# Keys, b's and receptances by token: 64x128 transposes in place of 64x64 products with an identity

## The chip, the cores and the metric

The kernel runs on one core of a Trainium2 chip. The metric is the device time of one execution in microseconds. A measurement is the median of several executions. Engines are called by the profile's names: PE is TensorE's matmul, PEld its weight load, DVE VectorE, ACT ScalarE, POOL GpSimd, SP SyncE, which issues most transfers.

## What is computed

One decoder block, for 16 meta tokens and 1024 tokens of width 1024: a half-step SwiGLU, a mixer with two branches (A: gated DeltaNet in chunks; B: RWKV-7), an output projection, another half-step SwiGLU, a norm. The change lies in branch B, whose reference is a recurrence over the tokens with one 64x64 state per head:

```python
def step(state, inp):
    r_t, w_t, k_t, v_t, a_t, b_t = inp
    sa = jnp.einsum('bhvk,bhk->bhv', state, a_t)
    state = state * w_t[:, :, None, :] + sa[..., None] * b_t[:, :, None, :] \
        + v_t[..., None] * k_t[:, :, None, :]
    return state, jnp.einsum('bhvk,bhk->bhv', state, r_t)
```

with `a_vec = -kk`, `b_vec = kk * a`, 16 heads of 64 channels.

## The kernel before

The kernel works in three parts: `ffn1`, `middle`, `ffn2`. `middle` holds both mixers. It takes the tokens in two segments (first 16 meta + 512 tokens, then 512) and the heads in eight groups `j`: two heads of branch B (128 partitions, one head in each half of them, `HS[0]` and `HS[1]`) and one head of branch A. So there are 16 iterations, 0 to 7 in segment 0 and 8 to 15 in segment 1. `schedule()` gives the order of the steps of an iteration; steps of three iterations stand side by side in it:

```python
REGULAR = "merge_blocks transitions operands+ inverses+ chains gates finish decay++ new_b++ new_a++"
```

That is the order in which the code is written. The framework's scheduler then gives each engine its own order, by data dependences, free buffers and its own idea of times; the projections (`pp`, three products per block of 128 rows) fill TensorE's order between the small products.

Branch B does not step through the tokens. It works on 8 chunks of 64 tokens (`NCB`, `CB`). `new_b` makes, with channels on the partitions, keys and b's scaled by decay (`BK`) and a-vectors and receptances scaled by decay (`AR`; `AR[:, :, 0]` is called "receptances" in the change's title, though it is made from `kkn`). `operands` multiplies them into the chunk matrices `LT` (tile `grb`), and turns them so that tokens are on the partitions:

- `bkt` (L1574): for each chunk, for `d` = 0, 1 and each head's half `h`, one 64x64 block of `BK` is multiplied with a 64x64 identity. The result goes to the partitions `HS[h ^ d]` of the bank `ps[d]`. ACT copies the two banks to `BKt` (L1577).
- `vp<-ck,AR` (L1342, in `run`): the same for `AR[..., 0, :]`, 16 products, copied to `at` (L1589); together with them, into the other half of the same two banks, 16 products `vp<-LT,Vs`, copied to `yb` (L1591).

`run` writes products of 64x64 blocks into up to two banks, one bank for blocks that stay on their half of the partitions and one for those that change it. `tok(i, h)` says on which half the tokens of chunk `i` of head `h` lie for the solve; `key(i, h)` is the other half. `transitions`, an iteration later, reads `BKt` and `at` block by block (tiles `xp`, `vp<-Vs,BKt`, `mp`, `np`), and `chains` runs the recurrences over the chunks (`p1`, `p2`, `pq`, `p3` for A, `b1` for B, `bq`). In segment 0 two more turns serve the meta tokens of branch A: `vmp` in `new_a` (L1483) and in `operands` (L1605), products of 16 columns with a 128x128 identity. The turns of A's full chunks (`vap` L1478, `ktp` L1600) are transposes already.

PSUM banks for these tiles come from the pool `mx`; `g.C(name)` is a slice of the constants' tile `ck`, and `g.sums` holds two 128x128 matrices (all ones, and ones in the two 64x64 blocks) by which column sums are taken.

## Time and profile before

| | us |
|---|---|
| median of 3 runs (2971.76 to 2984.48) | 2976.71 |
| the profiled execution | 2974.08 |
| its span, first to last instruction | 2972.3 |
| PE busy in the span | 2876.8 (97%) |
| DVE busy | 2208.8 (74%) |
| ACT busy | 1450.5 (49%) |
| POOL busy | 503.4 (17%) |
| mean granted TensorE clock | 0.993 |

In the rows that follow, `x64` is a number of instructions, `64*64` after an operation of TensorE is the part of the array that is used (rows by columns), and `64x64 f32` the operand. A busy time of a group counts overlapping instructions once. In the chain of work that ended last, the second number is the length of the piece.

### The profile page before, as it was taken

The page shows a single profiled execution, that of the slowest core. Times are in us where ns is not written, and L with a number is a line of the kernel's source. Part 1 is how long each engine was busy: PE and PEld are TensorE (multiplying, and loading weights), DVE is VectorE, ACT ScalarE, POOL GpSimd, SP SyncE. Part 2 cuts the span into 40 slices and gives each one's busy share as a digit, 9 for nine tenths or more (in the row PEclk, how much of TensorE's full clock was granted, in tenths as well). Part 3 has the DMA queues.
Part 4 walks back from the last instruction along what each step waited for, and adds up shares of the span by engine and source line. Part 5 has one row for each costly group of instructions (what it writes and reads, how often), then busy time and mean ns, then how long its engine had stood idle before and what let it go on. Part 6 is the DMA issues. An engine that isn't in the chain of part 4 may idle for free.

```text
span 2972.3 us, 63124 instructions
## 1 busy us (share of the span) xinstructions
PE 2876.8 (97%) x25720; PEld 2496.4 (84%) x25720; DVE 2208.8 (74%) x4121; ACT 1450.5 (49%) x2559; POOL 503.4 (17%) x578
## 2 busy tenths in 40 slices
PE   8999999999899999999998999999999999999998
PEld 8999999999878888888776777777777888888887
DVE  8666668776667877788878887778876766667886
ACT  6322234346555656565566556556644422223443
POOL 0332232323000000000000000001101032332431
PEclk9999999999999999999999999999999999999999
DMA  5333236553232322333232332333345332333763
GB/s 212 125 108 108 98 124 206 182 193 118 71 70 72 86 65 68 84 81 85 89 98 73 80 79 77 76 87 82 106 132 185 127 109 99 97 102 130 248 220 113
DMA packets 287907, 339.39 MB, mean 114 GB/s; under 512 B 172704, under 2 KB 181024, under 8 KB 287616
## 3 DMA queue, kind: packets, MB, share of 16 engines
q1 hardware_dynamic: 283600, 326.17, 36.0%
q0 software_dynamic: 2000, 6.56, 0.6%
q8 instruction: 202, 3.31, 0.5%
q10 hardware_dynamic: 2016, 2.63, 0.2%
q14 instruction: 89, 0.73, 0.1%
HBM read 267.63 MB, written 73.41 MB: 115 GB/s over the span
## 4 chain that ended last, share of the span: by engine, by line
PE 67%; DVE 19%; ACT 6%; issue 3%; DMA 3%; SPq 1%; POOL 0%; DVEq 0%; ACTq 0%; POOLq 0%
PE pg L521 25%; PE pp L315 15%; PE pd L742 10%; DVE w L164 3%; PE pwo L315 2%; PE pg L545 2%; DVE tb L1657 1%; DVE Xb L1659 1%; DVE form L164 1%; ACT w L163 1%; PE vp L1342 1%; DMA form<-frm 1%; PE mp L1342 1%; PE xp L1342 1%; PE np L1342 1%
## 5 line engine op out<-in xcount | busy, mean ns | idle before, releaser
L315 PE MATMUL pp<-uk,w 128*128 128x512 f32 (+2 forms) x4824 | 971.3, 347 | 13.8 <-DVE w L164 5.9
L315 PEld LDWEIGHTS pp<-uk,w 128*128 128x128 f32 x4824 | 745.4, 191 | 111.7 <-DVE w L164 14.7
L742 PE MATMUL pd<-form,w 128*128 128x256 f32 (+2 forms) x2904 | 437.3, 312 | 5.4 <-DVE w L164 5.2
L742 PEld LDWEIGHTS pd<-form,w 128*128 128x128 f32 x2904 | 402.7, 189 | 39.5 <-DVE w L164 7.3
L521 PE MATMUL pg<-bt,w 128*128 128x256 f32 (+2 forms) x2520 | 401.9, 318 | 3.1 <-DVE w L164 2.5
L521 PEld LDWEIGHTS pg<-bt,w 128*128 128x128 f32 x2520 | 360.2, 188 | 37.3 <-DVE w L164 3.8
L527 DVE TENSOR_TENSOR c<-c,pg 128x520 f32<-128x520 f32 (+1 forms) x280 | 189.4, 688 | 239.1 <-PE pg L521 215.8
L164 DVE TENSOR_TENSOR w<-wraw,w 128x1024 fp32r<-128x1024 f32 (+1 forms) x254 | 338.2, 1332 | 38.7 <-ACT w L163 37.1
L521 PE MATMUL pg<-b,w 128*128 128x256 f32 (+2 forms) x2160 | 348.1, 317 | 0.0
L163 ACT ACTIVATE w<-wraw 128x1024 fp32r<-128x1024 f32 (+1 forms) x254 | 266.9, 1052 | 164.1 <-PE pg L521 117.4
L521 PEld LDWEIGHTS pg<-b,w 128*128 128x128 f32 x2160 | 309.9, 188 | 28.3 <-DVE w L164 0.3
L163 ACT ACTIVATE w<-wrx 128x1024 fp32r<-128x1024 f32 (+1 forms) x64 | 58.4, 912 | 279.0 <-PE pg L521 239.2
L491 POOL TENSOR_TENSOR wrx<-wrx 128x512 f32<-128x512 f32 x38 | 52.5, 1381 | 612.8 <-DVE w22b L164 351.6
L164 DVE TENSOR_TENSOR form<-form 128x520 fp32r<-128x520 f32 (+1 forms) x152 | 145.8, 995 | 14.0 <-ACT form L163 13.8
L163 ACT ACTIVATE w<-wsum 128x768 fp32r<-128x768 f32 x96 | 75.6, 788 | 155.8 <-PE pd L742 117.1
L164 DVE TENSOR_TENSOR w<-wsum,w 128x768 fp32r<-128x768 f32 x96 | 112.9, 1181 | 37.3 <-ACT w L163 37.3
L163 ACT ACTIVATE form<-form 128x520 fp32r<-128x520 f32 (+1 forms) x152 | 93.8, 631 | 79.5 <-DMA form<-frm 73.4
L242 POOL TENSOR_TENSOR wsum<-wsum,wraw 128x768 f32<-128x768 f32 (+1 forms) x48 | 97.6, 2050 | 204.7 <-DMA wraw<-in_wdn 154.3
L1659 DVE TENSOR_TENSOR Xb<-Xb,tb 115x126 f32<-115x126 f32 (+22 forms) x496 | 125.2, 252 | 8.7
L1657 DVE TENSOR_TENSOR tb<-Ub,Xb 115x126 f32<-115x126 f32 (+22 forms) x496 | 124.5, 251 | 9.5 <-DMA Ub<-scr 2.0
L1466 DVE SCALAR_TENSOR_TENSOR acc<-xr,pk,acc 128x528 f32<-128x528 f32 (+1 forms) x144 | 109.0, 757 | 20.6 <-ACT acc L1462 19.9
L315 PE MATMUL pwo<-uk,w 128*128 128x512 f32 x384 | 95.3, 397 | 1.3 <-DVE uk L164 0.6
(439 smaller groups left out, 4421.4 us busy)
## 6 DMA issues: line engine op xcount, KB each, us to landing
wraw<-in_win SPq DMA_DIRECT2D x150, 512.0 KB
wraw<-in_wgu SPq DMA_DIRECT2D x44, 512.0 KB
wrx<-in_wgu SPq DMA_DIRECT2D x44, 512.0 KB
frm<-c SPq DMA_DIRECT2D x76, 260.0 KB
form<-frm SPq DMA_DIRECT2D x76, 260.0 KB
frm<-c SPq DMA_DIRECT2D x76, 256.0 KB
form<-frm SPq DMA_DIRECT2D x76, 256.0 KB
...
```

The costliest lines, as they stand in the source:

```text
L163: g.nc.scalar.activation(hi, src, AF.Copy)
L164: (eng or g.nc.vector).tensor_tensor(lo, src, hi.bitcast(F32), op=ALU.subtract)
L242: g.nc.gpsimd.tensor_tensor(s, x, y, op=ALU.add if r == 1 else ALU.subtract)
L315: g.last_product = g.nc.tensor.matmul(ps, lhsT=l, rhs=r, start=i == 0, stop=i == n - 1)
L521: nc.tensor.matmul(ps[:, c0 : c0 + cn], lhsT=l[:, x, k, :], rhs=r[:, k, y, c0 : c0 + cn], start=i == 0, stop=i == 3 * HK - 1)
L527: nc.vector.tensor_tensor(o, x, y, op=ALU.add)
L545: nc.tensor.matmul(ps[:, c0 : c0 + cn], lhsT=l[:, x, k, :], rhs=r[:, k, y, c0 : c0 + cn], start=i == 0, stop=i == 6 * HK - 1)
L742: nc.tensor.matmul(pd[:, c0 : c0 + cn], lhsT=wd[:, u, k - k0, :], rhs=x[:, v, c0 : c0 + cn], start=k + i == 0, stop=k == HF - 1 and i == 2)
L1342: g.nc.tensor.matmul(ps[e][HS[dst], c0 : c0 + CB], lhsT=l, rhs=r, start=True, stop=True)
L1466: nc.vector.scalar_tensor_tensor(acc[:, :n], xr[:, tap : tap + n], V("convw", ct * 4 + tap), acc[:, :n], op0=ALU.mult, op1=ALU.add)
L1657: nc.vector.tensor_tensor(tv, U[:, i, i + 1 :].unsqueeze(2).to_broadcast([npt, nt, ncc]), X[:, i, 0:ncc].unsqueeze(1).to_broadcast([npt, n ...
L1659: nc.vector.tensor_tensor(X[:, i + 1 :, 0:ncc], X[:, i + 1 :, 0:ncc], tv, op=ALU.add)
```

## The change

`BK` and `AR` lose the inner axis of two (b's and keys; a's and receptances). They become two runs of eight chunks with one more block of 64 columns between them, 17 blocks in all. POOL fills that block with three 64x64 copies per iteration, so that on the second head's half the chunks can also be taken in pairs that begin one block later. `turned` takes two neighbouring chunks of one half at a time, 64 rows by 128 columns, and transposes them into a 128x64 block: 16 transposes for `bkt`, 8 for `AR`. Bank `h` now holds head `h`. `place` and `turned_bk` find the blocks again in `transitions`. The two `vmp` products become transposes of 128 columns. The constant `bd` leaves `ck`; POOL makes the two matrices of `g.sums` with memsets, where DVE copied them.

```diff
@@ middle
-            nc.vector.tensor_copy(g.sums[x], g.C(x))
+            t = g.sums[x].bitcast(F32)
+            nc.gpsimd.memset(t, 0.0 if x == "bd" else 1.0)
+            if x == "bd":
+                for h in HS:
+                    nc.gpsimd.memset(t[h, h], 1.0)
...
+def place(i, h):
+    return (i - h) % NCB // 2
...
-def run(g, pool, name, *kinds):
-    ps, out, used = {}, [], [0, 0]
+def run(g, pool, name, *kinds, banks=()):
+    ps, out, used = dict(enumerate(banks)), [], [0, 0]
...
+def turned(g, ps, src, first):
+    for m in range(NCB // 2):
+        for h in range(2):
+            i = 2 * m + first[h]
+            g.nc.tensor.transpose(ps[h][:, m * CB : (m + 1) * CB], src[HS[h], i : i + 2].rearrange("p a m -> p (a m)"),
+                                  g.C("ident")[HS[h], HS[h]])
@@ new_b
-    BK = q.BK = st.tile([P, NCB, 2, CB], F32, name="BK", tag="BK")
-    nc.vector.tensor_tensor(BK[:, :, 1, :], ch3(k[:, fs], CB), ch3(EN[:, fs], CB), op=ALU.mult)
-    nc.vector.scalar_tensor_tensor(BK[:, :, 0, :], ch3(t1[:, fs], CB), -1.0, ch3(EN[:, fs], CB),
-                                   op0=ALU.mult, op1=ALU.mult)
-    AR = q.AR = st.tile([P, NCB, 2, CB], F32, name="AR", tag="AR", bufs=2)
-    nc.vector.tensor_tensor(AR[:, :, 0, :], ch3(kkn[:, fs], CB), ELx[:, :, 0:CB], op=ALU.mult)
+    BK = q.BK = st.tile([P, 2 * NCB + 1, CB], F32, name="BK", tag="BK")
+    ks, bs = BK[:, NCB + 1 :], BK[:, :NCB]
+    nc.vector.tensor_tensor(ks, ch3(k[:, fs], CB), ch3(EN[:, fs], CB), op=ALU.mult)
+    nc.gpsimd.tensor_copy(BK[HS[0], NCB], ks[HS[0], NCB - 1])
+    nc.vector.scalar_tensor_tensor(bs, ch3(t1[:, fs], CB), -1.0, ch3(EN[:, fs], CB), op0=ALU.mult, op1=ALU.mult)
+    nc.gpsimd.tensor_copy(BK[HS[1], NCB], bs[HS[1], 0])
+    AR = q.AR = st.tile([P, 2 * NCB + 1, CB], F32, name="AR", tag="AR", bufs=2)
+    nc.vector.tensor_tensor(AR[:, :NCB], ch3(kkn[:, fs], CB), ELx[:, :, 0:CB], op=ALU.mult)
+    nc.gpsimd.tensor_copy(AR[HS[1], NCB], AR[HS[1], 0])
@@ new_a (and the same in operands with kq[:, 0, 0:P])
-        nc.tensor.matmul(ps[:16, 0:P], lhsT=acc[:, 0:16], rhs=g.C("ident"), start=True, stop=True)
+        nc.tensor.transpose(ps[:, 0:P], acc[:, 0:P], g.C("ident"))
@@ operands
-    for i in range(NCB):
-        for d in range(2):
-            for h in range(2):
-                nc.tensor.matmul(ps[d][HS[h ^ d], i * CB : (i + 1) * CB], lhsT=BK[HS[h], i, d ^ (i & 1)],
-                                 rhs=ident[HS[h], HS[h]], start=True, stop=True)
-    for d in range(2):
-        nc.scalar.activation(BKt[:, :, d], ch3(ps[d], CB), AF.Copy)
+    turned(g, ps, BK, (0, 1))
+    turned(g, [p[:, FULL // 2 :] for p in ps], BK[:, NCB:], (0, 1))
+    for h in range(2):
+        nc.scalar.activation(BKt[:, :, h], ch3(ps[h], CB), AF.Copy)
...
+    banks = [g.mx.tile([P, 512], F32, name="vp", tag="mx") for _ in range(2)]
+    ps = [t[:, FULL // 2 :] for t in banks]
+    turned(g, ps, AR, (0, 1))
+    for h in range(2):
+        nc.scalar.activation(at[:, h * (NCB // 2) : (h + 1) * (NCB // 2)], ch3(ps[h], CB), AF.Copy)
...
-    pa, pr = run(g, g.mx, "vp", lambda i, h: (AR[HS[h], i, 0, :], ident[HS[h], HS[h]], h, tok(i, h)), vr)
-    for ps, cs in pa:
-        nc.scalar.activation(at[:, cs], ps, AF.Copy)
-    for ps, cs in pr:
+    for ps, cs in run(g, g.mx, "vp", vr, banks=banks)[0]:
         nc.scalar.activation(ch3(yb, CB)[:, cs], ps, AF.Copy)
@@ transitions (the blocks' new places)
+    def turned_bk(p, i, d):
+        h, s = p ^ d, d ^ (i & 1)
+        return BKt[HS[p], s * (NCB // 2) + place(i + s, h), h]
```

In the program order of each engine the change moves the following. In these rows numbers tell tiles of one name apart (after, `bkt_12167` and `bkt_12168` are the two banks), and `x8` counts products of the program.

TensorE in iteration 3 (segment 0), from the end of the small products for the meta tokens, before:

```order
L1808 MATMUL am_12422<-vnm,vkm 128x128
L1574 MATMUL bkt<-ck,BK 64x64 x32
L1815 MATMUL p_12427<-SA,kq 128x128
L1840 MATMUL b_12431<-SBs,mt 128x64
L315 MATMUL pp<-uk,w 128x512
L1342 MATMUL vp<-ck,AR 64x64 x16
L1342 MATMUL vp<-LT,Vs 64x64 x16
L1821 MATMUL p_12434<-rhA,Y_7680 128x128
L1840 MATMUL b_12436<-SBs,mt 128x64
```

and after:

```order
L314 MATMUL pp_12531<-uk_7559,w_12493 128x512
L1360 MATMUL bkt_12167<-ck_7211,BK_11563 128x64 x8
L314 MATMUL pp_12531<-uk_7603,w_12493 128x512
L1360 MATMUL bkt_12168<-ck_7211,BK_11563 128x64 x8
L1360 MATMUL vp_12188<-ck_7211,AR_11568 128x64 x4
L1838 MATMUL p1_12345<-SA_10946,kq_10297 128x128
L1863 MATMUL b1_12349<-SBs_12343,mt_7684 128x64
L314 MATMUL pp_12531<-uk_7603,w_12493 128x512
L1360 MATMUL vp_12189<-ck_7211,AR_11568 128x64 x4
L1350 MATMUL vp_12188<-LT_12058,Vs_11402 64x64 x7
```

Before, the 32 products stood together and mixed the two banks. The changed code writes the transposes of the two halves in turn; here all eight of bank 0 (the first head's half) come first and all eight of bank 1 behind a projection. The receptances' transposes stand four and four.

TensorE in iteration 10 (segment 1), behind the last `gra` of the same step, before:

```order
L1574 MATMUL bkt_19860<-ck_7211,BK_19374 64x64 x16
L1815 MATMUL p1_20033<-SA_18968,kq_18413 128x128
L315 MATMUL pp_20217<-uk_18047,w_20179 128x512
L1840 MATMUL b1_20037<-SBs_20031,mt_7684 128x64
L315 MATMUL pp_20217<-uk_18047,w_20179 128x512
L1574 MATMUL bkt_19861<-ck_7211,BK_19374 64x64 x16
L1342 MATMUL vp_19898<-ck_7211,AR_19377 64x64 x2
L1342 MATMUL vp_19899<-ck_7211,AR_19377 64x64 x2
```

and after:

```order
L1360 MATMUL bkt_20725<-ck_7211,BK_20236 128x64 x8
L1838 MATMUL p1_20874<-SA_19736,kq_19205 128x128
L314 MATMUL pp_21023<-uk_17893,w_20985 128x512
L1863 MATMUL b1_20878<-SBs_20872,mt_7684 128x64
L314 MATMUL pp_21023<-uk_17893,w_20985 128x512
L1360 MATMUL bkt_20726<-ck_7211,BK_20236 128x64 x8
L314 MATMUL pp_21023<-uk_17899,w_20985 128x512
L1360 MATMUL vp_20746<-ck_7211,AR_20241 128x64 x4
L314 MATMUL pp_21023<-uk_17899,w_20985 128x512
L1360 MATMUL vp_20747<-ck_7211,AR_20241 128x64 x4
```

Here two projections now stand between the second half of `bkt` and the two parts of `vp`, which had mixed before.

POOL in segment 1, one iteration's stretch from the copies that feed the inverses (`XA`) to the clearing of `Xb`, after (before, the same rows without the three 64x64 copies, and with `XA` behind the third `xr`):

```order
L1692 COPY XA<-Xc 32x4x32 [waits DMAHW6_49,Pool_49]
L1692 COPY XA<-Xc 32x4x32
L1449 COPY AR<-AR 64x64 [waits DVE_49]
L1480 COPY xr<-carA 128x3 [waits Pool_49]
L1446 COPY BK<-BK 64x64 [waits DVE_49,Pool_49]
L1480 COPY xr<-carA 128x3 [waits Pool_49]
L1444 COPY BK<-BK 64x64 [waits DVE_49]
L1480 COPY xr<-carA 128x3
L1669 MEMSET Xb 115x512 [waits DMAHW3_49,DMAHW2_49,PE_49]
```

The three copies stand between the copies of three columns into `xr`.

More of the change, by code (lines that the diff above doesn't have):

```diff
@@ L63 @@
 _c = 0
-for _n, _w in (("ones", 128), ("ident", 128), ("bd", 128), ("cmat", 128), ("mB", 128), ("mA", 128),
+for _n, _w in (("ones", 128), ("ident", 128), ("cmat", 128), ("mB", 128), ("mA", 128),
                ("mBm", 16), ("rsB", 528), ("sel", 16), ("rsA", 528)):
@@ L1434, in new_b @@
         nc.vector.scalar_tensor_tensor(g.bkm[:, 32:48], t1[:, 0:16], -1.0, EN[:, 0:16], op0=ALU.mult, op1=ALU.mult)
-    nc.vector.tensor_tensor(AR[:, :, 1, :], ch3(r[:, fs], CB), ELx[:, :, 1:], op=ALU.mult)
+    nc.vector.tensor_tensor(AR[:, NCB + 1 :], ch3(r[:, fs], CB), ELx[:, :, 1:], op=ALU.mult)
     bv = q.bv = st.tile([P, FULL], F32, name="bv", tag="bv", bufs=2)
@@ L1503, in operands @@
                 for h in range(2):
-                    nc.tensor.matmul(ps[d][HS[h ^ d], i * P : (i + 1) * P], lhsT=BK[HS[h], c4 + i, d ^ (i & 1)],
-                                     rhs=AR[HS[h], c4 + i].rearrange("p a b -> p (a b)"), start=True, stop=True)
+                    nc.tensor.matmul(ps[d][HS[h ^ d], i * P : (i + 1) * P], lhsT=BK[HS[h], (NCB + 1) * (d ^ (i & 1)) + c4 + i],
+                                     rhs=AR[HS[h], c4 + i :: NCB + 1][:, :2], start=True, stop=True)
         for d in range(2):
@@ L1604, in operands @@
         ps = g.mx.tile([P, 512], F32, name="vmp", tag="mx")
-        nc.tensor.matmul(ps[:16, 0:P], lhsT=kq[:, 0, 0:16], rhs=g.C("ident"), start=True, stop=True)
+        nc.tensor.transpose(ps[:, 0:P], kq[:, 0, 0:P], g.C("ident"))
         nc.scalar.activation(vkm[:, 1, :], ps[:16, 0:P], AF.Identity, scale=em[:, 1, 0:1])
@@ L1727, in transitions, with solved @@
     xa, xv = (st.tile([P, NCB, CB], F32, name=x, tag=x) for x in ("xa", "xv"))
-    vka = q.at
-    def solved(r):
+    vka, ar = q.at, AR[:, NCB + 1 :]
+    def solved(r, at=lambda i, h: i):
         def f(i, h):
             t = tok(i, h)
-            return Y[HS[t], i, HS[t]], r[HS[t], i], t, t
+            return Y[HS[t], i, HS[t]], r[HS[t], at(i, h)], t, t
         return f
@@ L1745, in va @@
         return LT[HS[k], i, 1 - (i & 1), :CB], Vs[HS[k], i], k, 1 - k
+    def turned_bk(p, i, d):
+        h, s = p ^ d, d ^ (i & 1)
+        return BKt[HS[p], s * (NCB // 2) + place(i + s, h), h]
     def vb(i, h):
         k = key(i, h)
-        return BKt[HS[k], i, 1 - (i & 1)], Vs[HS[k], i], k, h
-    px, pv = run(g, g.ch, "xp", solved(q.at), va)
+        return turned_bk(k, i, 1 - (i & 1)), Vs[HS[k], i], k, h
+    px, pv = run(g, g.ch, "xp", solved(q.at, lambda i, h: h * (NCB // 2) + place(i, h)), va)
     for ps, cs in pv:
@@ L1759, in transitions @@
         nc.scalar.activation(vbk[:, cs], ps, AF.Copy)
-    bt = lambda r, i: BKt[r, i, i & 1]
+    bt = lambda r, i: turned_bk(HS.index(r), i, i & 1)
     br = lambda r, i: LT[r, i, i & 1, CB:]
@@ L1848, in chains @@
         for hp in HS:
-            nc.tensor.matmul(ps[hp, i * CB : (i + 1) * CB], lhsT=SBs[hp, i], rhs=q.AR[hp, i, 1, :],
+            nc.tensor.matmul(ps[hp, i * CB : (i + 1) * CB], lhsT=SBs[hp, i], rhs=q.AR[hp, NCB + 1 + i],
                              start=True, stop=True)
@@ L1892, in finish @@
     nc.vector.scalar_tensor_tensor(oa, oa, V("aog"), zg, op0=ALU.mult, op1=ALU.mult)
-    sq = q.AR[:, 0:4].rearrange("p c y m -> p (c y m)")
+    sq = q.AR[:, :NCB].rearrange("p c m -> p (c m)")
     rg = st.tile([P, FULL], F32, name="rg", tag="ro")
```

3 lines of the change are left out of this document (1 added, 2 removed).

## The prediction

> **What bounds the kernel now.** I read the page first: its head, its busy row and the chain of work that ended last. Then the middle part alone, in two windows that lie inside segment 0 (iterations 2 to 7) and inside segment 1 (iterations 8 to 15).
>
> ```profile
> span 2972.3 us, 63124 instructions
> PE 2876.8 (97%) x25720; PEld 2496.4 (84%) x25720; DVE 2208.8 (74%) x4121; ACT 1450.5 (49%) x2559; POOL 503.4 (17%) x578
> PE 67%; DVE 19%; ACT 6%; issue 3%; DMA 3%; SPq 1%; POOL 0%; DVEq 0%; ACTq 0%; POOLq 0%
> ...
> 880.00:1450.00 570.00, 553.99 (x6789) 475.73 (x6788) 442.68 (x1098) 336.82 (x692) 37.03 (x133) 1.00 0.30 78
> 1560.00:2250.00 690.00, 660.87 (x7360) 524.95 (x7351) 541.91 (x1301) 402.16 (x768) 52.95 (x114) 0.99 0.34 90
> ```
>
> The first numbers of a window row are its length and PE's busy time in it. TensorE is busy 554 of 570 us and 661 of 690 us, at a granted clock of 1.00 and 0.99, and is two thirds of the chain. So an edit on TensorE counts where the chain runs over the edited products. The chain around them, in iteration 3 (segment 0) and in iteration 10 (segment 1); the second number is the piece's length:
>
> ```profile
> 1062.73 1.48 PE bkt L1574 x59
> 1064.21 0.42 PE p L1815 x2
> ...
> 1065.08 1.38 PE vp L1342 x59
> 1066.46 0.42 PE p L1821 x2
> ...
> 1068.16 0.59 PE ktp L1600 x4
> 1068.75 0.32 PE vmp L1605 x2
> 1069.07 0.42 PE pq L1827 x2
> 1069.49 0.22 PE pq L1828 x2
> ...
> 1071.56 0.22 PE p L1815 x2
> ```
>
> ```profile
> 1732.77 0.59 PE ktp L1600 x4
> 1733.36 0.22 PE p L1821 x2
> ```
>
> The products that the change replaces are on the chain without a gap: `bkt`, then a chunk of branch A (`p`), then `vp`. What TensorE spends there is paid in full, 16 times.
>
> **What the products cost now.** The same iterations in the timeline of TensorE (start, busy time, group), with the duration of a single one from the tile's own view:
>
> ```profile
> 1062.66 1.55 PE L1574 MATMUL bkt<-ck,BK 64*64 64x64 f32 x64
> ...
> 1065.01 0.92 PE L1342 MATMUL vp<-ck,AR 64*64 64x64 f32 x30
> 1065.73 0.27 PE L1342 MATMUL vp<-LT,Vs 64*64 64x64 f32 x2
> ```
>
> ```profile
> 1728.51 1.15 PE L1574 MATMUL bkt<-ck,BK 64*64 64x64 f32 x32
> ...
> 1730.69 0.97 PE L1574 MATMUL bkt<-ck,BK 64*64 64x64 f32 x26
> ...
> 1732.08 0.23 PE L1342 MATMUL vp<-ck,AR 64*64 64x64 f32 x2
> ```
>
> ```profile
> L1574 PE MATMUL bkt<-ck,BK x1024: 213/218/365, 787.7 to 2166.7; 64*64 64x64 f32 x171
> ```
>
> There are 1024 instructions where the program has 16 x 32 products: a float32 product is two passes, each with a load of its weights. One matmul is 218 ns long, but they overlap, so a stream costs its busy time less one 0.22. Segment 0: bkt 1.55 - 0.22 = 1.33 us, and the receptances' part of vp 1065.73 - 1065.01 = 0.72 us, together 2.05 us. Segment 1: first half of bkt 1.15 - 0.22 = 0.93 us; the other half runs into vp, from 1730.69 to 1732.08, 1.39 us; together 2.32 us. That is 96 instructions in 2.05 us, 21 ns each: four 64x64 corners of the array work side by side, or two where only one `bkt` tile is in turn (0.93 / 32 = 29 ns each).
>
> **The change, part by part.**
>
> *The transposes.* 32 + 16 products (96 instructions) become 16 + 8 transposes with 64 rows and 128 columns as weights and a 64x64 identity as the moving operand. A transpose is one instruction per product in this trace (ktp and vap: 4 per iteration in the program, 4 in the rows). No row has a 64-row, 128-column weight. The nearest with 128 columns:
>
> ```profile
> 1066.39 0.30 PEld L1821 LDWEIGHTS p<-rhA,Y 128*128 128x128 f32 x2
> 1066.61 0.30 PEld L1840 LDWEIGHTS b<-SBs,mt 128*128 128x128 f32 x2
> 1066.83 0.53 PEld L315 LDWEIGHTS pp<-uk,w 128*128 128x128 f32 x3
> ...
> 1714.30 0.60 PE L1478 MATMUL vap<-ck,acc 128*128 128x128 f32 x4
> ```
>
> The loads of p, b and pp begin 0.22 us apart, with two in each group: 0.11 us per pass, both for p, which moves 128 columns, and for b, which moves only 64. So the load of 128 columns sets the pace, not the moving side. The four transposes of vap take (0.60 - 0.27) / 3 = 0.11 us apart as well. I take 0.11 us for each of the 24, as long as they stand one behind the other on the same half of the rows. In the order of the changed program they do (shown in the section on the change, for iterations 3 and 10): all eight of one half, then all eight of the other, then four and four. 24 x 0.11 = 2.64 us: +0.59 us per iteration in segment 0, +0.32 in segment 1. The bounds: half of it, 0.055 each, if the halves could load side by side (as the corners do in the 29 ns row), 1.32 us; and nothing above 0.11, since a full 128 rows take no longer.
>
> *Going back to the full array.* p takes 0.42 us behind bkt and behind vp, and 0.22 us elsewhere (rows above): each return from 64-row tiles to the full array costs 0.20 us. Before there are two per iteration. After there are three in segment 0 (four in some iterations: I take 1.5 more, +0.30 us) and four in segment 1 (+0.40 us). New is a step from 64x128 tiles straight to the 64x64 tiles of `vp<-LT,Vs`; no row shows it. Between 0 (bkt and vp mix without a gap at 1730.69) and 0.20 I take 0.10 us.
>
> *The meta tokens' vmp* (segment 0 only). Its product has a 16-column tile; behind ktp it takes 0.32 and pq after it 0.42, while in segment 1 p follows ktp directly at 0.22. As a fifth transpose it should take 0.11 with pq at 0.22: -0.41 us. The other vmp, behind vap, 0.32 to 0.11: -0.21 us. Together -0.62 us.
>
> *POOL and DVE.* Three copies of 64x64 per iteration are added on POOL, which is 17% busy. The trace has a like copy, and one that falls into the very stretch of DVE work that they will fall into:
>
> ```profile
> L1836 POOL COPY SBs<-SB x16: 235/335/988, 884.7 to 2184.2; 128x64 f32<-128x64 f32 x16
> ```
>
> ```profile
> 1776.15 0.69 DVE L1429 TENSOR_TENSOR AR<-kkn,ELx 128x512 f32<-128x512 f32 x1
> 1776.75 0.68 DVE L1426 SCALAR_TENSOR_TENSOR BK<-t,sw 128x512 f32<-128x512 f32 x1
> 1776.97 1.24 POOL L1460 COPY xr<-carA 128x3 f32<-128x3 f32 x2 [14.35 <-DVE AR L1429]
> ...
> 1777.35 0.69 DVE L1423 TENSOR_TENSOR kB<-kB,av 128x512 f32<-128x512 f32 x1
> ...
> 1815.40 1.15 PE L1574 MATMUL bkt<-ck,BK 64*64 64x64 f32 x32
> ```
>
> The copies of three columns stretch to 0.6 us each, and the DVE instructions beside them keep their 0.68 to 0.69 us: POOL waits, DVE does not. What waits behind the copies on POOL are the copies into xr and XA, and on TensorE the transposes, 39 us later (BK is written at 1776.75 and transposed at 1815.40). I take 0 us; the upper bound is the whole 48 copies in DVE's time, 48 x 0.335 = 16 us, the lower one 0, since a copy added frees nothing. A rule weighs against me here: the Trainium skill, "SBUF — State Buffer", section "SBUF: two separate sides", says that a GpSimd instruction and a DVE instruction with two SBUF inputs exclude each other, and that whichever starts first keeps the shared ports until it ends. By it DVE would wait as often as POOL, and the sum would come near the upper bound; the rows above show only POOL waiting.
>
> DVE writes BK and AR in one piece now, not in 64-element runs: 0 us, as `AR` in runs and `kB` in one piece both take 0.69 us. Two DVE casts become four POOL memsets before the loop, and the constants' DMA loses 128 columns: once, hidden by the projections, below 1 us either way.
>
> *The sum.* Segment 0: 0.59 + 0.30 + 0.10 - 0.62 = +0.37 us; segment 1: 0.32 + 0.40 + 0.10 = +0.82 us. Eight iterations each: 3.0 + 6.6 = +9.6 us, all on the chain. The profiled execution took 2974.08 us (span 2972.3), 2.6 us under the median of the three runs, 2976.71. I forecast 2976.7 + 9.6 = 2986 us.
>
> **Rivals.**
> Faster: the halves overlap, or a 64-row load is quicker than a 128-row one, so that a transpose costs 0.055 us. The 24 take 1.32 us, 1.32 less than I counted; 16 x 1.32 = 21 us, and the time is 2986 - 21 = 2965 us. For it: the 21 ns row shows that small tiles do work side by side. Against it: they do so when neighbours in the order lie on different halves, which the order no longer gives. It decides from a price of 0.085 us per transpose, where the sum is zero. The Trainium skill, "TensorEngine Tiling (Array Packing)", section "Tiling Modes", has two 64x128 tiles that operate independently, which is this rival; by that page alone the time would be near 2965 us.
>
> Hidden: TensorE has 16 us of idle time in six iterations of segment 0 and 29 us in eight of segment 1, some of it just where the eviction of BKt is waited for. The first half's eviction can now start while the second half is transposed, and the longer work may fill what was idle. Then the time stays at 2977 us. Against it: bkt, p and vp follow on the chain without a gap.
>
> Slower: the 48 copies hold up DVE in the stretch where DVE is the chain. At 0.335 us each that is 16 us on top, 2986 + 16 = 3002 us. It needs more than 0.11 us per copy to pass the limit of 0.5%. Against it are the DVE rows at 1776 to 1778.
>
> **How the numbers follow.** Forecast 45%, between 2980 and 2993; faster rival 25%, 2959 to 2971; hidden 15%, 2974 to 2980; slower rival 15%, 2995 to 3004. A measurement of this kernel tells about 0.5% from no change, 14.9 us: below 2961.8 is faster, above 2991.6 slower. Faster holds two fifths of the faster rival, 0.10. Slower holds the slower rival and a fifth of the forecast, 0.24. The rest, 0.66, is the same. The range leaves a tenth on each side: 2963, two fifths into the faster rival, to 2999, in the middle of the slower one. The forecast's own range is 2980 to 2993.
>
> **What would show it.** In the profile after: bkt as 256 instructions with a stream of 0.77 us for eight neighbours (0.11 apart), and 0.055 in the one early iteration where the order mixes both halves if overlap exists; p at 0.42 behind each half; vmp at about 0.11 with pq at 0.22; DVE's AR and BK instructions still at 0.68 to 0.69 us, with no gaps behind them. The prediction is wrong if transposes of one half come less than 0.09 us apart, if the added time on TensorE disappears in idle time, or if another part of the order (projections stand differently between the small products) moves the period by more than these terms.

## The result: slower, and outside the range

The changed kernel takes 3007.33 us (median of four runs, 3003.85 to 3010.48), the kernel before 2974.24 (2967.73 to 2984.48, with one more run than was known at the prediction). The ratio is 1.0108, with a 95% interval of 1.0085 to 1.0131. The forecast was 2986, with a range up to 2999.

The page after, at the places shown of before, and the same two windows (segment 1 reaches to 2280 now):

```profile
span 3002.1 us, 60836 instructions
PE 2890.9 (96%) x24552; PEld 2505.1 (83%) x24552; DVE 2210.1 (74%) x4119; ACT 1454.9 (48%) x2559; POOL 528.0 (18%) x630
...
PE 70%; DVE 17%; ACT 5%; DMA 4%; issue 3%; POOL 1%; SPq 1%; DVEq 0%; ACTq 0%; POOLq 0%
```

```profile
880.00:1450.00 570.00, 549.04 (x6325) 474.19 (x6325) 438.25 (x1090) 336.94 (x689) 48.45 (x151) 1.00 0.30 78
1560.00:2280.00 720.00, 682.59 (x6855) 537.37 (x6852) 551.37 (x1310) 404.80 (x768) 57.33 (x135) 0.98 0.31 86
```

TensorE runs 1168 instructions fewer (24,552 against 25,720) and is busy 14 us longer. In segment 1 it was idle for 29 of 690 us and is now for 37 of 720, and the granted clock shows 0.98 where it was 0.99. That is no picture of products that cost more. Where the time arises is seen by cutting the trace at the first `bkt` of each iteration: iterations 10 to 14, five equal ones of segment 1, in one window each, before and then after.

```profile
1728.51:2163.63 435.12, 419.99 (x4701) 334.26 (x4700) 352.02 (x829) 263.81 (x504) 39.15 (x75) 1.00 0.32 85
```

```profile
1731.03:2191.98 460.95, 433.04 (x4341) 339.84 (x4340) 356.26 (x829) 266.16 (x504) 38.49 (x90) 0.97 0.30 80
```

These five take 25.8 us more, 5.2 each: 26 of the 29.8 us by which the span grew. Of the 25.8, 13.0 are busy time of TensorE (433.04 - 419.99) and 12.8 idle. Counted at the full clock, the busy time is what it was: 433.04 x 0.97 = 420. Up to iteration 10 the changed kernel is only 2.5 us late (1731.03 against 1728.51).

What the waits say: the group of the projections, `pp`, in the same five iterations (count, busy time and mean, then idle time ahead of them and what ended it), before and after.

```profile
L315 PE MATMUL pp<-uk,w 128*128 128x512 f32 x1080 | 282.0, 401 | 0.0
```

```profile
L314 PE MATMUL pp<-uk,w 128*128 128x512 f32 x1080 | 295.5, 412 | 19.9 <-ACT w L162 14.0 <-DVE w L163 5.9
```

The same 1080 products, which the change does not touch, now wait 19.9 us, 4.0 per iteration, for weights that ScalarE and VectorE split into two parts (`w<-wraw`). ScalarE's timeline in iteration 11 shows why, first before and then after:

```profile
1836.50 0.60 ACT L1211 ACTIVATE gg<-pp 128x512 f32<-128x512 f32 x1 [1.21 <-PE pp L315]
1836.99 1.05 ACT L163 ACTIVATE w<-wraw 128x1024 fp32r<-128x1024 f32 x1
...
1841.11 0.68 ACT L1370 ACTIVATE sw<-pw,pk 128x512 f32<-128x512 f32 x1
...
1847.63 1.04 ACT L163 ACTIVATE w<-wraw 128x1024 fp32r<-128x1024 f32 x1
```

```profile
1844.75 0.60 ACT L1214 ACTIVATE gg<-pp 128x512 f32<-128x512 f32 x1 [1.20 <-PE pp L314]
...
1848.42 0.68 ACT L1387 ACTIVATE sw<-pw,pk 128x512 f32<-128x512 f32 x1
...
1853.74 0.61 ACT L1401 ACTIVATE ELx<-Ls 128x512 f32<-128x512 f32 x1
1854.26 1.04 ACT L162 ACTIVATE w<-wraw 128x1024 fp32r<-128x1024 f32 x1
...
1855.78 1.04 ACT L162 ACTIVATE w<-wraw 128x1024 fp32r<-128x1024 f32 x1
...
1865.63 0.69 ACT L1205 ACTIVATE kB<-pp,pk 128x512 f32<-128x512 f32 x1 [8.42 <-PE pp L314]
```

Before, the split of the weight for B's keys (`kB`) stood right behind `gg`, 0.5 us after it began, ahead of the decay's activations (`sw` to `ELx`). After, it stands behind all of them, 9.5 us after `gg`, and the next split 1.5 us behind it. TensorE's timeline there:

```profile
1855.35 0.73 PE L314 MATMUL pp<-uk,w 128*128 128x512 f32 x2 [2.21 <-ACT w L162]
1856.87 0.73 PE L314 MATMUL pp<-uk,w 128*128 128x512 f32 x2 [0.79 <-ACT w L162]
1858.97 6.62 PE L314 MATMUL pp<-uk,w 128*128 128x512 f32 x22 [1.37 <-DVE w L163]
```

It waits 2.21 us for ScalarE's half, 0.79 for the next weight's, 1.37 for VectorE's half. Nothing in the diff touches this split. The order of each engine's instructions comes from a scheduler with estimates of its own, and with the small products changed it came out otherwise.

The changed products themselves, in iteration 11:

```profile
1823.30 0.71 PE L1360 MATMUL bkt<-ck,BK 64*128 64x64 f32 x8
1823.94 0.49 PE L1838 MATMUL p<-SA,kq 128*128 128x128 f32 x2
...
1825.05 0.71 PE L1360 MATMUL bkt<-ck,BK 64*128 64x64 f32 x8
1825.69 0.49 PE L314 MATMUL pp<-uk,w 128*128 128x512 f32 x1
1826.12 0.46 PE L1360 MATMUL vp<-ck,AR 64*128 64x64 f32 x4
1826.50 0.49 PE L314 MATMUL pp<-uk,w 128*128 128x512 f32 x1
1826.93 0.46 PE L1360 MATMUL vp<-ck,AR 64*128 64x64 f32 x4
1827.32 1.22 PE L1350 MATMUL vp<-LT,Vs 64*64 64x64 f32 x32
1828.47 0.66 PE L1619 MATMUL ktp<-ck,kq 128*128 128x128 f32 x4
```

Eight transposes take 0.71 - 0.22 = 0.49 us from the first start to the last; by the single starts 0.11 us for the first step and 0.062 for each of the others, where 0.11 was forecast for all. But the 32 products `vp<-LT,Vs` that follow take 1.15 us to the next group's start: two of them start together every 0.058 us. Before, they took about half; there the products of both banks mix (iteration 12, 0.56 us from the start of these 30 to that of `ktp` at 1906.51):

```profile
1905.85 0.28 PE L1342 MATMUL vp<-LT,Vs 64*64 64x64 f32 x2
1905.95 0.63 PE L1342 MATMUL vp<-LT,Vs 64*64 64x64 f32 x30
```

### The profile page after: what moved, and what is told of

Read it like the earlier page. It is cut to its first block, busy times and chain, and to the rows that moved or that the text cites. A ratio compares the mean times of both kernels' runs of the same rounds, so it can differ in the third digit from the quotient of the medians.

```text
span 3002.1 us, 60836 instructions
## 1 busy us (share of the span) xinstructions
PE 2890.9 (96%) x24552; PEld 2505.1 (83%) x24552; DVE 2210.1 (74%) x4119; ACT 1454.9 (48%) x2559; POOL 528.0 (18%) x630
## 4 chain that ended last, share of the span: by engine, by line
PE 70%; DVE 17%; ACT 5%; DMA 4%; issue 3%; POOL 1%; SPq 1%; DVEq 0%; ACTq 0%; POOLq 0%
PE pg L520 24%; PE pp L314 19%; PE pd L741 8%; DVE w L163 3%; PE pwo L314 2%; DVE tb L1676 2%; PE pg L544 1%; DVE form L163 1%; DVE Xb L1678 1%; DMA form<-frm 1%; PE vp L1350 1%; ACT w L162 1%; PE xp L1350 1%; PE cs L1292 1%; PE mp L1350 1%
## 5 line engine op out<-in xcount | busy, mean ns | idle before, releaser
L314 PE MATMUL pp<-uk,w 128*128 128x512 f32 (+2 forms) x4824 | 989.3, 350 | 37.2 <-DVE w L163 18.4
L163 DVE TENSOR_TENSOR w<-wsum,w 128x768 fp32r<-128x768 f32 x96 | 111.6, 1168 | 36.7 <-ACT w L162 36.5
L162 ACT ACTIVATE form<-form 128x520 fp32r<-128x520 f32 (+1 forms) x152 | 94.2, 632 | 80.8 <-DMA form<-frm 75.6
L314 PE MATMUL pwo<-uk,w 128*128 128x512 f32 x384 | 95.3, 397 | 1.3 <-DVE uk L163 0.6
```

Of the source, the lines that this page charges most:

```text
L162: g.nc.scalar.activation(hi, src, AF.Copy)
L163: (eng or g.nc.vector).tensor_tensor(lo, src, hi.bitcast(F32), op=ALU.subtract)
L314: g.last_product = g.nc.tensor.matmul(ps, lhsT=l, rhs=r, start=i == 0, stop=i == n - 1)
```

## The experiments

Theory: the late split makes nearly all of the loss, and the transposes by themselves save a little. Rivals: the transposes with their switches, GpSimd's copies or new layouts, the queue of SyncE. Each kernel ran against the kernel before on the same chip, and its ratio is to that; the medians in the table come from several chips. The table has the start of `bkt` in four iterations, from TensorE's timeline, the end of the span, and two periods worked out from them: segment 0 = (iteration 7 - iteration 3) / 4, segment 1 = (iteration 15 - iteration 10) / 5.

| kernel | median us | it. 3 | it. 7 | it. 10 | it. 15 | span | seg. 0 | seg. 1 |
|---|---|---|---|---|---|---|---|---|
| before | 2974.24 | 1062.66 | 1439.54 | 1728.51 | 2163.63 | 2972.3 | 94.2 | 87.0 |
| after | 3007.33 | 1061.39 | 1442.45 | 1731.03 | 2191.98 | 3002.1 | 95.3 | 92.2 |
| 1 early fetch | 2981.41 | 1060.91 | 1444.49 | 1733.10 | 2168.00 | 2980.5 | 95.9 | 87.0 |
| 2 late split in before | 2999.61 | 1059.23 | 1436.25 | 1736.22 | 2190.94 | 2998.1 | 94.3 | 90.9 |
| 3 products, new layout | 2977.05 | 1061.40 | 1438.44 | 1728.66 | 2163.36 | 2973.6 | 94.3 | 86.9 |
| 4 keys and b's only | 2965.86 | 1054.50 | 1429.24 | 1720.53 | 2151.27 | 2961.9 | 93.7 | 86.1 |
| 5 alternating | 2970.83 | 1063.77 | 1443.08 | 1728.87 | 2158.18 | 2971.6 | 94.8 | 85.9 |
| 6 receptances only | 2975.76 | 1060.74 | 1439.43 | 1725.27 | 2160.45 | 2974.3 | 94.7 | 87.0 |
| 7 meta products only | 2978.22 | 1060.02 | 1437.73 | 1728.08 | 2163.39 | 2976.3 | 94.4 | 87.1 |
| 8 keys and b's, alternating | 2962.59 | 1056.84 | 1432.29 | 1718.50 | 2147.22 | 2953.3 | 93.9 | 85.7 |
| 9 store moved | 3010.98 | 1063.11 | 1447.28 | 1738.85 | 2202.55 | 3012.1 | 96.0 | 92.7 |
| 10 transposes twice | 2976.11 | 1065.13 | 1444.57 | 1734.66 | 2167.87 | 2980.1 | 94.9 | 86.6 |
| 11 as 8, meta as before | 2962.61 | 1057.68 | 1434.13 | 1718.63 | 2147.44 | 2956.2 | 94.1 | 85.8 |
| 12 half filled | 3017.32 | 1059.85 | 1441.80 | 1740.04 | 2202.08 | 3016.9 | 95.5 | 92.4 |
| 13 filled | 3011.02 | 1062.68 | 1444.34 | 1740.82 | 2198.47 | 3009.1 | 95.4 | 91.5 |

From iteration 15 to the end, where the kernels differ in that one iteration's products alone, the profiled executions spread from 806 to 815 us (8: 2953.3 - 2147.22; 12: 3016.9 - 2202.08). So single differences of a few microseconds in the whole are not read; the periods are. Those of segment 1 repeat from one iteration to the next. In segment 0 the order of some kernels changes between iterations, and with it which products a cut takes in: from iteration 2 to 6 experiment 4 has 94.6 us and experiment 5 94.3, where the table has 93.7 and 94.8. Differences of such kernels there are not read.

**1 and 2: the split alone.** Experiment 1 is the changed kernel with the next weight fetched and split in `finish`, one step sooner in the program:

```diff
@@ finish
     oa, yb, zg, gg = q.oa, q.yb, q.zg, q.gg
     sq = q.Va.rearrange("p c m -> p (c m)")
+    if q.s and q.it < 2 * NJ - 2:
+        fetchw(g)
```

> The changed kernel, transposes and all, with one edit: in segment 1 the weight for B's keys is fetched and split one step sooner in the program (in finish, ahead of the decay), so that its split stands on ScalarE ahead of the decay's activations, as it does in the kernel before. Theory (the late split is the loss): the iterations of segment 1 last 86 to 88 us again in place of 92.2, and the whole is 2962 to 2980 us. Rival (the transposes, their switches of tile form, or the copies on GpSimd are the loss): the period stays at 91 to 92 us and the whole at 3000 or more.

Measured: 2981.41 us (2973.07 to 2991.41), ratio 1.0029 (1.0017 to 1.0042), a microsecond above the range. Segment 1 is back at 87.0 us, and the projections wait for nothing:

```profile
L314 PE MATMUL pp<-uk,w 128*128 128x512 f32 x1080 | 283.4, 401 | 0.0
```

Experiment 2 is the kernel before, with only that split held behind the decay's last activation on ScalarE (an order, no wait):

```diff
+        late = g.late if name == "win" and 40 <= idx[0] < 48 else []
...
-    split(g, src, w[:, 0, :kk, :], w[:, 1, :kk, :])
+    with ExitStack() as after:
+        for x in [] if down else late:
+            after.enter_context(g.tc.issue_after(x.ins))
+        split(g, src, w[:, 0, :kk, :], w[:, 1, :kk, :])
...
-    nc.scalar.activation(ELx[:, :, 1:], ch3(Ls[:, fs], CB), AF.Exp, scale=-CDEC)
+    elx = nc.scalar.activation(ELx[:, :, 1:], ch3(Ls[:, fs], CB), AF.Exp, scale=-CDEC)
+    g.late = [elx] if q.s and it < 2 * NJ - 1 else []
```

> The kernel before, with its 64x64 products, and one edit: in segment 1 ScalarE's split of the weight for B's keys is held behind the decay's last activation, where it stands in the changed kernel. Theory (the late split is the loss): the iterations of segment 1 last 91 to 93 us in place of 87, and the whole is 3000 to 3012 us, though nothing is transposed. Rival (transposes or copies): 2970 to 2982 us, since the split is hidden as before.

Measured: 2999.61 us (2999.12 to 3003.47), ratio 1.0090 (1.0075 to 1.0105), half a microsecond under the range. Without one transposing, four of the five iterations last 91.3 to 92.1 us (the last, 87.6, has its split early again), and the waits are of the changed kernel's kind, 13.6 us of its 19.9:

```profile
L319 PE MATMUL pp<-uk,w 128*128 128x512 f32 x1080 | 294.1, 412 | 13.6 <-ACT w L163 11.0 <-DVE w L164 2.6
```

```profile
1736.22:2190.94 454.72, 431.56 (x4701) 340.31 (x4701) 354.04 (x829) 263.70 (x504) 29.68 (x75) 0.97 0.30 81
```

The two runs together show it: take the late split out and segment 1's loss goes; put it in alone and most of it comes (4.3 to 5.1 of 5.2 us in the four iterations that have it).

**9: which queue.** In the changed kernel a weight's fetch also moved behind the store of the iteration's result on SyncE's queue: in iteration 11 it is issued at 1858.95, behind the store at 1857.63; before, at 1839.33, ahead of the store at 1849.29. Experiment 9 takes that store away from there:

```diff
-        nc.sync.dma_start(g.mdr[q.s][j], yb)
+        nc.gpsimd.dma_start(g.mdr[q.s][j], yb)
```

> The changed kernel with one edit: the store of each iteration's result is issued by GpSimd in place of SyncE, so that the fetches of weights no longer stand behind it on SyncE's queue; the order on ScalarE, VectorE's split included, and on TensorE stays that of the changed kernel. Theory (the split's place on ScalarE, behind the decay, is what TensorE waits for): segment 1 stays at 91.5 to 92.5 us an iteration, the whole 3000 to 3010 us. Rival (the store on SyncE's queue delayed the fetch, and the fetch the split): segment 1 at 87 to 88, the whole 2975 to 2988.

Measured: 3010.98 us (3003.53 to 3022.63), ratio 1.0117 (1.0094 to 1.0140), 92.3 to 93.6 us an iteration, a microsecond above both bands. Freeing the queue does not help; the place on ScalarE decides. The moved fetch is not that of the weight split late: the one ahead of it was issued at 1836.54, and the moved one starts where VectorE's half of the late split ends (1857.71 + 1.22 = 1858.93), so it follows the split.

**3, 4, 6 and 7: one part at a time.** Experiment 3 keeps the layouts, the copies and the constants, and undoes every transposing:

```diff
-    turned(g, ps, BK, (0, 1))
-    turned(g, [p[:, FULL // 2 :] for p in ps], BK[:, NCB:], (0, 1))
+    for i in range(NCB):
+        for d in range(2):
+            for h in range(2):
+                nc.tensor.matmul(ps[d][HS[h ^ d], i * CB : (i + 1) * CB], lhsT=BK[HS[h], (NCB + 1) * (d ^ (i & 1)) + i],
+                                 rhs=ident[HS[h], HS[h]], start=True, stop=True)
...
-    for ps, cs in run(g, g.mx, "vp", vr, banks=banks)[0]:
+    pa, pr = run(g, g.mx, "vp", lambda i, h: (AR[HS[h], i], ident[HS[h], HS[h]], h, tok(i, h)), vr)
```

> The changed kernel with its layouts of 17 blocks, its three copies on GpSimd in each iteration and its constants, but B's keys, b's and receptances by token again by 64x64 products, and the two meta products by a plain product. Theory (late split, which here stands where it does before): 2970 to 2982 us, within 0.3% of before. Rival (the copies on GpSimd or the new layouts hold VectorE or TensorE): 2990 to 3007 us. By the forecast's own terms, which put the copies at nothing: 2974 plus 0 to 2.

Measured: 2977.05 us (2972.49 to 2985.66), ratio 1.0016 (1.0004 to 1.0029); both periods are those of before. Copies and layouts are not the loss.

Experiment 4 makes only the second half of this edit: the receptances go by products again, keys and b's and the meta products stay transposed.

> The changed kernel with keys and b's transposed (16 transposes in each iteration), and the receptances by token again by 64x64 products. The weight's split stands in segment 1 where it does in the kernel before. Theory (late split; a transpose starts 0.062 us after the one before it, so 16 of them take 1.0 us where 32 products took 1.4 to 1.6): 2962 to 2976 us, at or a little under before. Rival (transposes and their switches cost TensorE time, by the forecast's 0.11 us each): 2980 to 2986 us.

Measured: 2965.86 us (2960.57 to 2975.60), ratio 0.9975 (0.9964 to 0.9986): 0.9 us less per iteration in segment 1, which alone makes 7 us. In segment 0 the two cuts disagree. Transposing keys and b's gains.

Experiment 6 makes only the first half, so that keys and b's go by products, and has the early fetch of experiment 1. The meta products stay transposed here too:

> Only the receptances by token are transposed (8 transposes in each iteration, keys and b's by products), with the earlier fetch in segment 1. The split stands ahead of the decay in segment 1, but in segment 0 its order is in five iterations the one that the changed kernel has in two (split ahead of the first gate's activation; those two lasted 96.7 where 94.1 stood before). Theory: segment 1 at 87 to 88 us, since the 64x64 products behind these transposes run two at a time (1.15 us in place of 0.57); segment 0 at 96 to 97 in iterations 2 to 6; the whole 2983 to 2994 us. Rival (the moved split is harmless in segment 0): segment 0 at 94 to 95, the whole 2973 to 2981.

Measured: 2975.76 us (2970.41 to 2982.13), ratio 1.0009 (0.9994 to 1.0024). The theory's part on segment 0 fell: 94.7 us, not 96 to 97, so the order that I had blamed there does not cost 2 us. The 96.7 was half of a pair: in the changed kernel iterations of 93.6 and 96.7 us alternate, with 1044 and 1062 products of TensorE between the cuts. Segment 1, 87.0, is as expected. Transposing the receptances brings nothing there; in segment 0 it costs 0.5 us together with the meta products, which alone cost 0.2 (experiment 7).

Experiment 7 is the kernel before with the two meta products transposed:

```diff
-        nc.tensor.matmul(ps[:16, 0:P], lhsT=acc[:, 0:16], rhs=g.C("ident"), start=True, stop=True)
+        nc.tensor.transpose(ps[:, 0:P], acc[:, 0:P], g.C("ident"))
...
-        nc.tensor.matmul(ps[:16, 0:P], lhsT=kq[:, 0, 0:16], rhs=g.C("ident"), start=True, stop=True)
+        nc.tensor.transpose(ps[:, 0:P], kq[:, 0, 0:P], g.C("ident"))
```

> The kernel before with one part of the change: the two meta products of each iteration of segment 0 as full transposes. Forecast's term: 0.62 us less in each of 8 iterations, 2968 us (2966 to 2971). Rival (TensorE does not wait there, or the order gives it back): 2971 to 2977.

Measured: 2978.22 us (2973.84 to 2986.82), ratio 1.0018 (1.0002 to 1.0034), above the rival's range too; segment 0 at 94.4 for 94.2. No gain. From iteration 3 to 7, before and then in experiment 7:

```profile
1062.66:1439.54 376.88, 366.11 (x4505) 315.14 (x4504) 294.26 (x727) 224.41 (x459) 24.75 (x83) 1.00 0.31 80
1060.02:1437.73 377.71, 364.66 (x4498) 315.58 (x4497) 294.27 (x728) 224.16 (x460) 19.48 (x83) 1.00 0.30 80
```

TensorE is busy 1.45 us less (366.11 - 364.66) and idle 2.3 us more (13.05 for 10.77), so what the rows save is lost in waits.

**5, 8, 10 and 11: what a transposing costs.** Experiment 5 writes out the order on TensorE, each small product behind the one that the code lists ahead of it:

```diff
-            g.nc.tensor.transpose(ps[h][:, m * CB : (m + 1) * CB], src[HS[h], i : i + 2].rearrange("p a m -> p (a m)"),
-                                  g.C("ident")[HS[h], HS[h]])
+            with ExitStack() as after:
+                if g.step:
+                    after.enter_context(g.tc.issue_after(g.step.ins))
+                g.step = g.nc.tensor.transpose(ps[h][:, m * CB : (m + 1) * CB], src[HS[h], i : i + 2].rearrange("p a m -> p (a m)"),
+                                               g.C("ident")[HS[h], HS[h]])
```

(and the same in `run` for the products that follow in these banks).

> The changed kernel, all three transposed, with TensorE's order within the small groups written out: transposes alternate between the upper and the lower 64 rows, and the 64x64 products that follow alternate between their two banks, as the code lists them. (In segment 1 of the changed kernel eight transposes of one row half follow each other, 0.062 us apart, and then 7, 8 and 1 products of one bank, 0.03 us each; in segment 0, where row halves alternated by chance, two transposes started within 0.062 us.) With this order the weight's split stands ahead of the decay in both segments. Theory (order alone was the loss, and transposes are cheap where row halves alternate): segment 1 at 84.8 to 86.2 us an iteration, the whole 2948 to 2966 us. Rival (transposes cost what two at a time cost as well): segment 1 at 87 us, the whole 2972 to 2982.

Measured: 2970.83 us (2965.42 to 2976.89), ratio 0.9988 (0.9973 to 1.0003). Segment 1, at 85.9, is where the theory put it; the whole is 5 us above its range. Experiment 8 does the same to experiment 4:

> Keys and b's transposed, receptances by products, and the transposes alternate between row halves by a written order. Theory: 16 transposes in 0.6 to 0.8 us where eight of one half and eight of the other took 1.27: segment 1 at 85.4 to 86.1 us in place of 86.3, the whole 2955 to 2964 us. Rival (the order within the group does nothing): 2963 to 2969 as without it.

Measured: 2962.59 us (2955.10 to 2973.22), ratio 0.9967 (0.9952 to 0.9981); segment 1 at 85.7. In its timeline, 15 transposes in alternation (the first stands apart) take as long as eight of one half did:

```profile
1806.65 0.71 PE L1364 MATMUL bkt<-ck,BK 64*128 64x64 f32 x15
1807.29 0.50 PE L314 MATMUL pp<-uk,w 128*128 128x512 f32 x1
```

Experiment 10 makes each of these transposes twice:

```diff
     turned(g, [p[:, FULL // 2 :] for p in ps], BK[:, NCB:], (0, 1))
+    turned(g, ps, BK, (0, 1))
+    turned(g, [p[:, FULL // 2 :] for p in ps], BK[:, NCB:], (0, 1))
```

> The kernel with keys and b's alone transposed in alternation, and each of its 16 transposes made twice (32 in each iteration, the second over the first in the same place). If a transposing costs TensorE 0.031 us where row halves alternate (the pairs' spacing in the traces so far), 0.5 us more in each of 16 iterations: 2967 to 2974 us. At 0.062 each, 1.0 us more: 2975 to 2981. At the forecast's 0.11, 1.8 us more: 2988 to 2994. Hidden behind other engines: 2960 to 2965.

Measured: 2976.11 us (2969.98 to 2981.86), 13.5 more than experiment 8, within the band of 0.062 us each.

```profile
1824.02 1.22 PE L1364 MATMUL bkt<-ck,BK 64*128 64x64 f32 x31
1825.17 0.68 PE L1351 MATMUL vp<-ck,AR 64*64 64x64 f32 x16
```

On TensorE 16 more take 1.15 - 0.64 = 0.51 us, 0.032 each, as the first theory has it; the iterations of segment 1 grew by 0.9 us. The rest comes with an order that moved again: the receptances' products stand by bank now, 16 and then 14, where experiment 8 mixed them, and the `vp` group takes 1.78 us (1825.17 to 1826.95) in place of 1.35 (1807.72 to 1809.07). The two, 0.51 and 0.43 us, make the 0.9. A price worked out from the whole alone would have been 0.053 us, too high by two thirds.

Experiment 11 leaves the meta products of experiment 8 as they were before:

> Keys and b's alone transposed in alternation, and the two meta products left as plain products. If the full transposes of the meta products bring nothing in the place where they stand, 2957 to 2965 us. By the forecast's term of 0.62 us in each of 8 iterations they did: 2966 to 2970.

Measured: 2962.61 us (2955.03 to 2966.55), ratio 0.9951 (0.9934 to 0.9968). It lies in the range that was given for meta transposes that bring nothing: they gain nothing there. With experiment 8 it is the fastest, ahead of both kernels.

**12 and 13: why a wait of 4 us costs 5.** The clock after the stall in iteration 11 of the changed kernel, by windows (the number before the last two is the granted clock):

```profile
1853.50:1859.00 5.50, 1.49 (x5) 0.62 (x5) 5.41 (x13) 3.72 (x7) 0.19 (x1) 0.95 0.11 41
1859.00:1861.00 2.00, 2.00 (x5) 1.61 (x6) 2.00 (x4) 0.00 (x0) 0.00 (x0) 0.50 0.55 171
1861.00:1863.00 2.00, 2.00 (x9) 1.60 (x8) 1.83 (x9) 0.00 (x0) 0.00 (x0) 0.78 0.71 236
1863.00:1865.50 2.50, 2.50 (x12) 1.81 (x10) 2.02 (x10) 0.00 (x0) 0.00 (x0) 1.00 0.45 169
```

From the stall's last gap on TensorE runs at half its clock (in iterations 10 and 13 from within its first gap on). The stretch lasts 3.41 us here and in two more of the five iterations, and 6.82 us in the two others; one of each:

```profile
1858.46:1861.87 3.41, 2.90 (x7) 2.32 (x8) 3.38 (x9) 0.00 (x0) 0.00 (x0) 0.50 0.65 229
2039.37:2046.19 6.82, 5.38 (x11) 3.37 (x12) 6.79 (x17) 2.12 (x5) 0.00 (x0) 0.50 0.33 115
```

Does the clock fall because of the stall? Experiment 12 gives TensorE useless work in the first gap:

```diff
+    if c.s and 40 <= ct < 48:
+        for _ in range(8):
+            g.nc.tensor.matmul(ps, lhsT=c.u[0][:, 0, 0:P], rhs=c.u[0][:, 0, :FULL], start=True, stop=True)
```

> The changed kernel, late split and all, with eight extra products of 512 columns in each iteration of segment 1, ahead of the product for B's keys and written over by it: TensorE works through 1.9 us of the 2.2 us in which it waited for the split. Nothing else is due there, so the extra work costs nothing by itself. In the changed kernel the granted clock falls to 0.50 for about 3 us behind each of these stalls (its 0.97 over the five iterations makes 13 of the 26 us lost there). Theory (the stall is paid a second time through the clock): the clock stays at 0.99 to 1.00 in these iterations, they last 89 to 90.5 us in place of 92.2, and the whole is 2988 to 2997 us, with more work than before. Rival (the clock does not hang on the stall): 92 us, the whole 3003 to 3012.

Measured: 3017.32 us (3013.39 to 3018.65), ratio 1.0138 (1.0115 to 1.0162), 92.4 us an iteration, clock 0.98. A miss, above the rival's range too: the gaps that were left (0.41, 0.78 and 1.37 us) still halved the clock in four of the five iterations. In the first, with gaps of 0.37, 0.78 and 1.38 us, it stayed at 1.00, and that iteration is the shortest; the first two:

```profile
1740.04:1830.97 90.93, 86.72 (x877) 68.32 (x876) 71.21 (x167) 53.29 (x101) 7.94 (x18) 1.00 0.29 78
1830.97:1924.55 93.58, 89.35 (x877) 70.21 (x876) 71.43 (x167) 53.30 (x101) 8.04 (x18) 0.96 0.28 76
```

The other three last 92.4 to 92.6 us. Experiment 13 fills these too, with 13 products by zeros behind the first two (`g.pad` is 13 for B's keys in segment 1, else 0):

```diff
+            if i == 2:
+                for _ in range(g.pad):
+                    g.nc.tensor.matmul(ps, lhsT=g.upz[HS[1], 2, :], rhs=hi[HS[1]], start=False, stop=False)
```

> The kernel with eight filling products before B's keys, and 13 more behind its first two products: they add products with zeros to the sum, 3.1 us of TensorE's time in the 3.6 us between the first two products and the third (in the run with eight alone, a pair of another product and 2.2 us of waiting stood there, and the clock still fell to 0.50 behind it). TensorE now waits less than 0.6 us in all at this place, and the weight comes as late as before. Theory (a stall is paid a second time through the clock): the clock stays at 0.99 to 1.00 over the five iterations, they last 89.2 to 90.8 us in place of 92.4, and the whole is 2993 to 3006 us. Rival (the clock falls for another reason than TensorE's waiting): 92 to 93 us an iteration, clock 0.97 to 0.98, the whole 3012 to 3020.

Measured: 3011.02 us (3010.03 to 3016.30), ratio 1.0127 (1.0109 to 1.0144).

```profile
1955.97 0.73 PE L314 MATMUL pp<-uk,w 128*128 128x512 f32 x2 [0.41 <-ACT w L162]
1956.63 3.26 PE L318 MATMUL pp<-uk,upz 64*128 64x512 f32 x13
1959.82 5.29 PE L314 MATMUL pp<-uk,w 128*128 128x512 f32 x22
```

```profile
1740.82:2198.47 457.65, 447.47 (x4446) 353.26 (x4446) 355.94 (x829) 266.19 (x504) 41.96 (x90) 1.00 0.30 81
```

The clock holds at 1.00, so it is TensorE's idling that lets it fall. When it falls, the traces show further: all changes of the clock in one profile lie whole multiples of 3.413 us apart (after, the falls at 1762.89, 1858.46, 1950.62, 2039.37 and 2134.94 are 28, 27, 26 and 28 such steps apart). In the step ahead of these falls TensorE waited 1.9 to 2.0 us, ahead of the four in experiment 12 1.6 to 2.2, and in that run's first iteration at most 1.5 in one step. So the sum of the waits in a step seems to count, and where the steps happen to lie. It is not the whole rule: in experiment 1 the clock fell at 1348.0 with no wait in the step before.

But the iterations last 91.5 us, 0.9 under experiment 12 and not the 1.6 to 3.2 that I expected, and the whole is 5 us above the range. (Iterations 8 and 9 together take 6 us more in experiment 13 and 9 us more in 12 than in the changed kernel, which neither expectation counted.) The clock is the smaller part of the loss: without its fall 3.9 to 4.5 of the 5.2 us remain (90.9 and 91.5 us against 87.0). The larger part goes with the product for B's keys, which ends late, so that ScalarE's and VectorE's chain from `kB` on starts late. That this chain is what lengthens the iteration is read from the starts, not tested by itself. In the iteration from 1915.46 (after) the first `vbp`, behind that product, starts at 42.2 us and `bon` at 57.0; in experiment 1 (from 1907.08) they start at 35.5 and 52.6, and in experiment 13 (from 1923.92) still at 41.1 and 56.5.

## Why the prediction was wrong, step by step

- **The step that failed is the order on the engines that the diff does not name.** The sum took the moves on TensorE between the small products and the copies on GpSimd, and left ScalarE's order unread. There the split of a weight had gone behind the decay: 5.2 us in each of five iterations, 26 of 29.8. The text named "another part of the order" as what would make it wrong, gave it no price, and looked for it on TensorE alone.
- **The transposes, 0.11 us each: wrong.** Eight of one half start 0.062 us apart, and alternating halves two in that time, 0.031 each (experiments 8 and 10). The first is near the faster rival's 0.055, by the second of its two grounds, a 64-row load quicker than one of 128 rows; the first ground, halves side by side, shows only where they alternate. There the trace agrees with the two independent 64x128 tiles of the Trainium skill, "TensorEngine Tiling (Array Packing)", section "Tiling Modes" (15 transposes in 0.64 us in experiment 8). Per iteration 24 x (0.11 - 0.062) = 1.15 us were counted too much. The rows I chose as nearest had 128 rows of weights, and I held 64 rows to be no faster.
- **The step to `vp<-LT,Vs`, 0.10 us: too small.** The step itself is short, but the 32 products lost their partners: 1.15 us in place of some 0.6. They now stand by bank, and two start together every 0.058 us; before, 30 started within 0.41 us (0.63 - 0.22), four in 0.055. That is 0.5 to 0.6 us per iteration that the sum did not have, and it takes back half of what the cheap transposes saved. In segment 1 with the split in its place (experiment 1) all of it together came to 0.0 us where +0.82 was forecast. That experiment 1's whole lies 8.6 us above before, close to the forecast's +9.6, is therefore luck: of the 6.6 us that segment 1 was to add, none came.
- **Returns to the full array, 0.20 us each: right.** A lone projection between two groups takes 1826.12 - 1825.69 = 0.43 us, against 5.29 / 22 = 0.24 in a stream (experiment 13, from 1959.82).
- **vmp, -0.62 us per iteration: the rows came as forecast, the gain did not.** The transposing takes 0.11 us and `pq` behind it 0.22:

```profile
1067.33 0.27 PE L1624 MATMUL vmp<-ck,kq 128*128 128x128 f32 x1
1067.44 0.39 PE L1850 MATMUL pq<-kq,SA 128*128 128x128 f32 x2
```

  Yet segment 0 with this part alone (experiment 7) is 0.2 us longer: TensorE's waits grow by more than its rows shrink. Which order makes them grow was not isolated.
- **GpSimd's copies, 0 us: right within what can be told.** VectorE's instructions beside them keep their length, GpSimd's stretch, and experiment 3 has the periods of before:

```profile
L1448 DVE TENSOR_TENSOR AR<-kkn,ELx x16: 680/686/779, 746.3 to 2152.7; 128x512 f32<-128x512 f32 x16
L1449 POOL COPY AR<-AR x16: 264/642/1187, 747.1 to 2153.6; 64x64 f32<-64x64 f32 x16
```

  By the forecast's reading of the rule that it weighed (the Trainium skill, "SBUF — State Buffer", section "SBUF: two separate sides"), VectorE would have waited as often as GpSimd. GpSimd's waits agree with that rule; no row here shows VectorE waiting in its turn: the longest of its 16 instructions lies 0.09 us over their median, the longest copy 0.55 over its own. The result lies near the 3002 us of the slower rival, but not by its mechanism.
- **Segment 0, +0.37 us per iteration: measured +1.05** ((1442.45 - 1061.39) / 4 against 94.2), and all of it is waiting. From iteration 3 to 7 after, against the row of before at experiment 7:

```profile
1061.39:1442.45 381.06, 365.62 (x4209) 315.81 (x4208) 293.67 (x728) 224.95 (x459) 35.30 (x95) 1.00 0.29 78
```

  TensorE is busy 365.62 us for 366.11, so the terms of the sum, which are all busy time, come to -0.1 us per iteration; it is idle 15.4 us for 10.8. The sum had no term for waits. Among the new ones are `pp` for VectorE's half of a weight (2.3 us for 0.7) and `iv` for a fetch of `Xc` (2.2 for 0). Why they grow stays open, as does which estimate made the scheduler move the split. Of the 8.6 us by which experiment 1 stays above before, 5 lie ahead of iteration 7 (there its profile has 6.8 us at half clock in iteration 6, from 1348.0) and 4 behind iteration 15, where the spread of all kernels is as large.
- **The chances** were read off their ranges too generously: spread evenly, 2961.8 us lies a quarter of the way into the faster rival's range, not two fifths, and a ninth of the forecast's lies above 2991.6, not a fifth. This changes nothing in the outcome.
